# A two-layer diffusion block on TensorE: tile positions, warm matmuls and fp32 modulation sums

## The chip, the cores and the metric

The kernel runs on one core of a Trainium2 chip. The metric is the device time of one execution in microseconds; the median of several runs is compared. TensorE (PE) multiplies matrices and transposes, VectorE (DVE), ScalarE (ACT) and GpSimd (POOL) work on elements, and the transfers from memory run on 16 DMA engines. Two queues issue nearly all transfers: SyncE's (SP), with the weights of the products, and GpSimd's, with the modulation weights and small tables.

## The reference

Two layers of a block over 256 latent and 256 context tokens of width 1024. Each has two sub-layers: a token mixer of three branches (retention, neighbourhood attention, grouped-query attention), merged with gates and projected, and an MLP of width 4096 with a squared ReLU. Every sub-layer is normalised ahead and behind, and modulated by six vectors per layer (two shifts, two scales, two gates), for the latent from c and for the context from c_ctx. The second layer computes the context only as far as the latent reads it. The output is the latent stream.

```
for l in range(2):
    sh1, sc1, gt1, sh2, sc2, gt2 = split(silu(c) @ w_mod[l] + b_mod[l])     # context: the same from c_ctx
    h = rms_norm(x, g_pre_mix[l]) * (1 + sc1) + sh1
    y, yc = token_mixer(h, hc, ...)                                          # w_in, branches, w_br, w_out
    x = x + gt1 * rms_norm(y, g_post_mix[l])
    h = rms_norm(x, g_pre_mlp[l]) * (1 + sc2) + sh2
    x = x + gt2 * rms_norm(square(relu(h @ w_mlp_in[l])) @ w_mlp_out[l], g_post_mlp[l])
    # layer 0 does the same for the context
```

## The kernel before

**Products.** Every large product is computed from two parts of each operand, a high part rounded to fp32r and the rest, in three fp32r matmuls: high by high, high by low, low by high (`mm3`, line 184). The weights come as tiles of 512 KB on SP's queue (`wload`, line 224), ScalarE copies the high part `wh`, and VectorE subtracts for the low part `wl` (`wsplit`, line 230). `wr`, `wh` and `wl` have three buffers each, which are taken in turn. One weight tile is one step of TensorE: 24 matmuls of 512 columns (512 tokens, or 512 weight columns), or 24 of 256 where only the latent is left. In the records such a matmul is named by its output: `ps` (projections and the first MLP product; the weights are held in the array and hT moves), `pO` (second MLP product and w_out; weights move), `pB` and `br` (weights move too).

**Where tiles lie.** Each pool lies behind the one before it in a partition: constants, a pad of `PAD` fp32 columns, 31 S tiles of 4096 bytes (`S`, all large activations: hT, u, yT, z, X, acc), 8 T tiles of 2048 bytes, small tiles, a second pad, the weight buffers. With the sizes declared before, S and T tiles begin 256 bytes past a multiple of 512. A `wh` or `wl` buffer has 1056 columns, 4224 bytes, which is 128 past a multiple of 512; so the three buffers of `wh` begin at 256, 384 and 0 and those of `wl` at 128, 256 and 384. For 256-wide products the weights begin 64 bytes into their buffer (`odd`).

**Order.** Steps are written as a list, and a scheduler orders the instructions of each engine by a modelled timeline with that list as priority. Some are pinned: `Ordered` (line 61) keeps the program's order for instructions issued while it is on, `issue_after` holds an instruction behind another. `HLD` = 2 holds the splits of the first two weight tiles of layer 1's MLP behind `st["xn_ins"]`, the last multiply of the norm.

**Start of layer 1's MLP.** After the last step of w_out (`pO<-wh,yT`), `post` (line 539) updates X per 128 tokens with a chain of eight small VectorE operations (`qv`, `qy`, `qa`). `pre_sq` squares X on ScalarE for each 128 tokens, `pre_xn` (line 499) runs one chain of 14 small operations (`pv`, `py`, `pa`) for both, then multiplies twice: z = X·y. `pre_tr` transposes z on TensorE (16 matmuls into `ph`), `pre_h` makes hT from it, and the MLP's first products follow.

**Modulation sums.** `mod_dve` (line 401) computes one vector: eight tiles `mr` of 128 weight rows come on GpSimd's queue, and VectorE accumulates them into `acc`, one S tile per stream. The first accumulation adds `brow`, a constant tile that is zero but for row 0, into which the bias is written by a transfer. What is left is the sum over the 128 partitions. `fin1` splits `acc` into `ahi` and `alo`. For a gate `fin2` sums with a matrix of ones. For the other vectors it multiplies with `oneh` (a column of ones at the stream's place) into `pmr`, two rows for the two streams, per half of 512 columns; ScalarE copies the two rows to `r`, and `fin3` transposes them by four tiny matmuls per half (`pm<-ident,r`) so that the vector lies along the partitions. Six vectors are non-gates: four for both streams, two for the latent alone. The steps of the modulation are woven between steps of the mixer and of the MLPs.

Of the kernel before, what the change touches and what calls it, by code (L numbers as in the profile page):

```python
# [42 lines left out]
PEO = ((99, 99), (99, 99))  # L43
HLD = 2
GAPF = 0
MPE = False
# [5 lines left out]
PLD = 4  # L52
PAD, PAD2 = 16, 16
FILL = (((0, 9), (9, 21), (21, 33)), ((0, 9), (7, 22), (22, 39)))
# [27 lines left out]
def kernel(  # L82
# [120 lines left out]
    cs = const.tile([128, 8, 2], F32, tag="cs", name="cs")  # L203
    brow = const.tile([128, 2, 512], F32, tag="brow", name="brow")
    ones = const.tile([128, 128], F32R, tag="ones", name="ones")
    oneh = const.tile([128, 2, 128], F32R, tag="oneh", name="oneh")
    onesf = const.tile([128, 128], F32, tag="onesf", name="onesf")
# [11 lines left out]
    def wtile(pool, tag, name, odd=False):  # L219

        t = pool.tile([128, 1056], F32R, tag=tag, name=name)
        return t[:, 16:1040] if odd else t[:, 0:1024]
# [20 lines left out]
    def prologue():  # L243
# [29 lines left out]
        def init():  # L273
            msr = S("msr")
            v_.tensor_copy(msr[:, 0, :], brow[:, 0, :])
            v_.tensor_copy(msr[:, 1, :], brow[:, 0, :])
            msr = msr.rearrange("p a b -> p (a b)").rearrange("p (k m) -> p k m", k=8)
            v_.tensor_copy(msr[:, :, 0:2], cs)
            tt(msr[:, :, 2:4], cs, f(msr[:, :, 0:2]), ALU.subtract)
            M["msr"] = msr  # L280
            for n_ in ("sh1", "sc1"):
                st[0, n_] = smp.tile([128, 8, 2], F32, tag=n_, name=n_, bufs=2)
            pr.extend(mmt(f"pr{i}") for i in range(4))
# [117 lines left out]
    def mod_dve(l, vec, streams):  # L401
# [10 lines left out]
        def fin2():  # L412
            if gate:
                for s in streams:
                    G = S(f"G{s}", F32)
                    st[l, name, s] = G
                    for half in range(2):
# [8 lines left out]
                        tt(G[:, half, :], pg, st["gb", half], ALU.mult)  # L426
                return
            ns = len(streams)
            M["r"] = []
            for half in range(2):  # L430
                ps = att("pmr")
                for s in streams:
                    for p in range(2):
                        t_.matmul(ps, oneh[:, s, :], M[s][p][:, half, :],
                                  start=(s == 0 and p == 0), stop=(s == ns - 1 and p == 1))
                r = T("r2")
                s_.copy(r[0:2, :], ps[0:2, :])
                M["r"].append(r)

        def fin3():  # L440
            o = smp.tile([128, 8, 2], F32, tag=name, name=name, bufs=2)
            st[l, name] = o
            pt = att("pm")
            for half in range(2):
                for j in range(4):
                    jj = 8 * half + 2 * j
                    t_.transpose(pt[:, jj:jj + 2], M["r"][half][0:2, 128 * j:128 * j + 128], ident[0:2, 0:2])
            pt3 = pt[:, 0:16].rearrange("p (j e) -> p j e", e=2)
            for s in streams:
                if vec in (0, 3):  # L450
                    v_.tensor_copy(o[:, :, s], pt3[:, :, s])
                else:
                    stt(o[:, :, s], pt3[:, :, s], 1.0, gp[:, 2 * l + vec // 3, :], ALU.add, ALU.mult)

        def step(kc):
            def go(ws):
                w = mrp.tile([128, 2, 512], F32, tag="mr", name="mr")
                nc.gpsimd.dma_start(  # L458
                    out=w, in_=w_mod[l, 128 * kc:128 * kc + 128, vec * D:vec * D + D].rearrange("p (a n) -> p a n", a=2))
                if kc == 0:  # L460
                    nc.gpsimd.dma_start(out=brow[0:1], in_=b_mod[l:l + 1, vec * D:vec * D + D].rearrange("o (a n) -> o a n", a=2))
                for s in streams:
                    if kc == 0:
                        st["acc", s] = S("acc", F32)
                    a = st["acc", s]
                    stt(a, w, cs[:, kc, s:s + 1], brow if kc == 0 else a, ALU.mult, ALU.add)
            return go

        fins = [fin1, fin2] if gate else [fin1, fin2, fin3]
        o = [([], step(kc)) for kc in range(8)]  # L470
# [28 lines left out]
    def pre_xn(s, sq):  # L499
        ms, z = sq  # L500
        X = st["X"]
        y = stats(ms, 2, EPS, "p")
        st["xn", s] = []
        for t in range(2):
            st["xn_ins"] = v_.tensor_scalar_mul(out=z[t], in0=X[2 * s + t], scalar1=y[:, t:t + 1])
            st["xn", s].append(z[t].rearrange("p a b -> p (a b)"))
# [767 lines left out]
    def setup():  # L1274
# [3 lines left out]
        nc.gpsimd.dma_start(out=sel, in_=sel_in)  # L1278
        v_.memset(brow, 0.0)
        th = sm("cth", 8, 2)  # L1280
# [4 lines left out]
    def setup2():  # L1285
# [9 lines left out]
        v_.tensor_copy(ones, onesf)  # L1295
        v_.tensor_copy(oneh[:, 0, :], brow[:, 0, 0:128])
        v_.tensor_copy(oneh[:, 1, :], brow[:, 0, 0:128])
        v_.tensor_copy(oneh[:, 0, 0:1], onesf[:, 0:1])
        v_.tensor_copy(oneh[:, 1, 1:2], onesf[:, 0:1])

# [60 lines left out]
    pb = pre_steps(1, 1, 0)  # L1361
    steps += pb[:1] + ([([], barrier)] if HLD else []) + pb[1:]
    if MPE:
# [139 lines left out]
```

## Time and profile before

| what | value |
|---|---|
| runs, us | 1471.29, 1471.39, 1478.82 |
| median, us | 1471.39 |
| profiled execution, us | 1478.93 |
| its span, us | 1477.2 |
| granted TensorE clock, mean | 0.990 |
| PE busy, us (share) | 1427.6 (97%) |
| DVE busy, us (share) | 1079.4 (73%) |
| ACT busy, us (share) | 747.1 (51%) |

The span goes from the first to the last instruction of the profiled execution; its own time is 1.7 us longer. Matmuls follow each other more closely than the duration of one record, so that a pace is read from starts or from windows, not from a mean duration. A granted clock of 1.00 is the higher of TensorE's two levels, 2.4 GHz; 0.50 is 1.2 GHz.

### The profile page before, as it was taken

Reading aid. Unit: us, or ns where it says so; the run is one execution under the profiler, and the core shown is the slowest. Engines: PE = TensorE matmul, PEld = TensorE weight load, DVE = VectorE, ACT = ScalarE, POOL = GpSimd, SP = SyncE. Lnnn points to the kernel's source line nnn. Section 1 sums busy time; section 2 is a strip of 40 time slices with the busy share of each in tenths; the row PEclk is TensorE's granted clock in tenths of the full one; section 3 lists DMA queues with packets and bytes.
Section 4 is the critical chain, followed back from the end, with each engine's and each line's share of the span. In section 5 each row is a group of like instructions: output and inputs, shape, how many; then the busy total and the mean of one; then the engine's idle time right before and its main releaser. Section 6 shows DMA issues by size and latency. Waiting matters only on the chain. (4 is left out here: it accounts for less than half of the span.)

```text
span 1477.2 us, 20910 instructions
## 1 busy us (share of the span) xinstructions
PE 1427.6 (97%) x7926; PEld 1212.9 (82%) x7926; DVE 1079.4 (73%) x1999; ACT 747.1 (51%) x1259; POOL 67.8 (5%) x131
## 2 busy tenths in 40 slices
PE   4999999999999999999999999999999999799997
PEld 4878788877788889988888887788889999699886
DVE  5785797787998669967755647986877886766544
ACT  5563565554323347625335155665546655576542
POOL 2000000000110000100001100000000000000000
PEclk9999999999999999999999999999999999899999
DMA  8622121222566556846546647443233445387653
GB/s 287 197 72 72 44 72 58 83 70 91 171 188 183 157 200 174 251 144 188 159 135 218 198 119 235 144 124 95 72 94 107 150 140 189 113 227 215 209 185 119
DMA packets 231957, 219.64 MB, mean 149 GB/s; under 512 B 7652, under 2 KB 188956, under 8 KB 231856
## 3 DMA queue, kind: packets, MB, share of 16 engines
q1 hardware_dynamic: 217856, 170.42, 37.4%
q0 software_dynamic: 14000, 47.88, 10.6%
q8 instruction: 62, 1.02, 0.3%
q14 instruction: 39, 0.32, 0.1%
HBM read 217.22 MB, written 1.05 MB: 148 GB/s over the span
## 5 line engine op out<-in xcount | busy, mean ns | idle before, releaser
L73 PE MATMUL ps<-hT,wh 128*128 128x256 f32 (+1 forms) x2480 | 602.4, 335 | 1.6 <-ACT wh L73 1.6
L73 ACT CAST wh<-wr 128x1024 fp32r<-128x1024 f32 x295 | 309.2, 1051 | 449.9 <-PE ps L73 180.9
L73 DVE TENSOR_TENSOR wl<-wr,wh 128x1024 fp32r<-128x1024 f32 x295 | 359.7, 1223 | 211.7 <-ACT wh L73 211.4
L73 PEld LDWEIGHTS ps<-hT,wh 128*128 128x128 f32 x2480 | 419.1, 190 | 55.5 <-issue 6.6
L73 PE MATMUL ps<-hT,wl 128*128 128x256 f32 (+1 forms) x1240 | 415.2, 335 | 5.1 <-DVE wl L73 4.9
L73 PEld LDWEIGHTS ps<-hT,wl 128*128 128x128 f32 x1240 | 234.9, 189 | 29.2 <-DVE wl L73 6.1
L73 PE MATMUL pO<-wh,u 128*128 128x512 f32 x768 | 241.7, 394 | 0.0
L73 PEld LDWEIGHTS pO<-wh,u 128*128 128x128 f32 x768 | 144.1, 188 | 33.7
L73 DVE SCALAR_TENSOR_TENSOR acc<-mr,cs,acc 128x1024 f32<-128x1024 f32 x112 | 141.2, 1282 | 28.9 <-DMA mr<-in_w_mod_dram 28.4
L73 PE MATMUL pO<-wl,u 128*128 128x512 f32 x384 | 151.2, 394 | 0.2 <-DVE wl L73 0.2
L73 PEld LDWEIGHTS pO<-wl,u 128*128 128x128 f32 x384 | 72.1, 188 | 16.6 <-DVE wl L73 0.6
L73 PE MATMUL pB<-wh,hT 128*128 128x512 f32 x256 | 82.9, 394 | 0.0
L458 POOL DMA_DIRECT2D mr<-in_w_mod_dram x80 | 42.6, 533 | 647.4 <-DVE acc L73 618.5
L73 PE MATMUL pO<-wh,yT 128*128 128x512 f32 x192 | 60.3, 393 | 0.0
L73 PEld LDWEIGHTS pB<-wh,hT 128*128 128x128 f32 x256 | 48.1, 188 | 10.6
L73 DVE TENSOR_TENSOR PT<-pt,PT 128x512 fp32r<-128x512 f32 x80 | 51.5, 682 | 2.8 <-ACT PT L73 2.2
L73 PE MATMUL pB<-wl,hT 128*128 128x512 f32 x128 | 50.3, 393 | 0.0
L73 ACT CAST PT<-pt 128x512 fp32r<-128x512 f32 x80 | 43.2, 599 | 8.5 <-PE pt L73 6.5
L73 PE MATMUL pt<-ident,P 128*128 128x128 f32 x320 | 42.0, 273 | 0.8 <-DVE P L73 0.6
L73 PEld LDWEIGHTS pO<-wh,yT 128*128 128x128 f32 x192 | 35.9, 188 | 8.2
L73 DVE TENSOR_TENSOR u<-rl,u 128x256 fp32r<-128x256 f32 (+1 forms) x71 | 36.7, 517 | 7.4 <-ACT u L73 7.4
L73 DVE TENSOR_SCALAR P<-P,su 128x512 f32<-128x512 f32 (+1 forms) x96 | 40.3, 440 | 1.6
(261 smaller groups left out, 1909.6 us busy)
## 6 DMA issues: line engine op xcount, KB each, us to landing
wr<-in_w_m_dram SPq DMA_DIRECT2D x143, 512.0 KB, 4.5
wr<-in_w_in_dram SPq DMA_DIRECT2D x104, 512.0 KB, 3.7
mr<-in_w_mod_dram POOLq DMA_DIRECT2D x80, 512.0 KB, 4.5
wr<-in_w_br_dram SPq DMA_DIRECT2D x24, 512.0 KB, 3.4
wr<-in_w_out_dram SPq DMA_DIRECT2D x24, 512.0 KB, 3.7
pr<-in_w_mod_dram SPq DMA_DIRECT2D x16, 512.0 KB, 6.3
bt<-in_relb_dram POOLq DMA_DIRECT2D x16, 192.0 KB, 2.7
X<-in_x_dram SPq DMA_DIRECT2D x4, 512.0 KB, 4.9
```

The lines of the kernel that those rows point to most:

```text
L73: ins = call(*a, **k)
L458: nc.gpsimd.dma_start(out=w, in_=w_mod[l, 128 * kc:128 * kc + 128, vec * D:vec * D + D].rearrange("p (a n) -> p a n", a=2))
```

## The change

Four things are done at once. After the last step of w_out in layer 1, `keep_warm` issues 64 matmuls of 256 columns (ones by a tile of yT) into a PSUM tile that nobody reads; the last w_out step, these matmuls and the following transposes are pinned in program order on TensorE. `pre_xn` computes the norm's chain for each 128 tokens by itself, each followed by its multiply, in all its uses. For the non-gate vectors of the modulation `fin1` is gone: `fin2` multiplies `acc` in fp32 with a matrix of 32 columns whose first is ones, one matmul per stream and half, each into a group of 32 PSUM partitions; one ScalarE copy takes all rows, and `fin3` transposes 64 or 128 rows at a time and picks the columns. The bias row lies in an S tile that GpSimd clears for each vector. And the positions change: the constants lose 4992 bytes, `PAD` grows by 1664, `PAD2` by 1024, and `wh` and `wl` buffers by 384 bytes each, so that S and T tiles begin at multiples of 2 KB and all weight buffers at multiples of 512 bytes (256-wide weights still 64 bytes further).

```diff
--- before.py
+++ after.py
@@ -42,6 +42,7 @@
 SWAP = (0, 1)
 PEO = ((99, 99), (99, 99))
 HLD = 2
+WARM1 = 64
 GAPF = 0
 MPE = False
 M1A, M1B = 8, 40
@@ -50,7 +51,7 @@
 ORD = ((0, 4, 5), (0, 4, 8))
 RW = 2
 PLD = 4
-PAD, PAD2 = 16, 16
+PAD, PAD2, WP = 432, 272, 1152
 FILL = (((0, 9), (9, 21), (21, 33)), ((0, 9), (7, 22), (22, 39)))
 PLAN = ["c4 t0 a0 c5 r0 f0 h0 c9 g0 c13",
         "a1 t1 r1 c14 f1 h1 c18",
@@ -201,9 +202,8 @@
     selr = const.tile([4, 512], F32R, tag="selr", name="selr")
     cc = const.tile([128, 8, 2], F32, tag="cc", name="cc")
     cs = const.tile([128, 8, 2], F32, tag="cs", name="cs")
-    brow = const.tile([128, 2, 512], F32, tag="brow", name="brow")
     ones = const.tile([128, 128], F32R, tag="ones", name="ones")
-    oneh = const.tile([128, 2, 128], F32R, tag="oneh", name="oneh")
+    oneh = const.tile([128, 32], F32, tag="oneh", name="oneh")
     onesf = const.tile([128, 128], F32, tag="onesf", name="onesf")
     gp = const.tile([128, 4, 8], F32, tag="gp", name="gp")
     gq_gain = const.tile([128, 4], F32, tag="gain", name="gain")
@@ -218,7 +218,7 @@
 
     def wtile(pool, tag, name, odd=False):
 
-        t = pool.tile([128, 1056], F32R, tag=tag, name=name)
+        t = pool.tile([128, WP], F32R, tag=tag, name=name)
         return t[:, 16:1040] if odd else t[:, 0:1024]
 
     def wload(spec):
@@ -272,8 +272,10 @@
 
         def init():
             msr = S("msr")
-            v_.tensor_copy(msr[:, 0, :], brow[:, 0, :])
-            v_.tensor_copy(msr[:, 1, :], brow[:, 0, :])
+            zero = T("zero")
+            v_.memset(zero, 0.0)
+            v_.tensor_copy(msr[:, 0, :], zero)
+            v_.tensor_copy(msr[:, 1, :], zero)
             msr = msr.rearrange("p a b -> p (a b)").rearrange("p (k m) -> p k m", k=8)
             v_.tensor_copy(msr[:, :, 0:2], cs)
             tt(msr[:, :, 2:4], cs, f(msr[:, :, 0:2]), ALU.subtract)
@@ -425,32 +427,34 @@
                         t_.matmul(pg, ones, M[s][1][:, half, :], start=False, stop=True)
                         tt(G[:, half, :], pg, st["gb", half], ALU.mult)
                 return
+
             ns = len(streams)
-            M["r"] = []
+            ps = att("pmr")
             for half in range(2):
-                ps = att("pmr")
                 for s in streams:
-                    for p in range(2):
-                        t_.matmul(ps, oneh[:, s, :], M[s][p][:, half, :],
-                                  start=(s == 0 and p == 0), stop=(s == ns - 1 and p == 1))
-                r = T("r2")
-                s_.copy(r[0:2, :], ps[0:2, :])
-                M["r"].append(r)
+                    j = 32 * (ns * half + s)
+                    t_.matmul(ps[j:j + 32, :], oneh, st["acc", s][:, half, :], start=True, stop=True)
+            for s in streams:
+                st.pop(("acc", s))
+            r = M["r"] = T("r2")
+            s_.copy(r[0:64 * ns, :], ps[0:64 * ns, :])
 
         def fin3():
             o = smp.tile([128, 8, 2], F32, tag=name, name=name, bufs=2)
             st[l, name] = o
             pt = att("pm")
-            for half in range(2):
-                for j in range(4):
-                    jj = 8 * half + 2 * j
-                    t_.transpose(pt[:, jj:jj + 2], M["r"][half][0:2, 128 * j:128 * j + 128], ident[0:2, 0:2])
-            pt3 = pt[:, 0:16].rearrange("p (j e) -> p j e", e=2)
+            ns = len(streams)
+            R = 64 * ns
+            for j in range(4):
+                t_.transpose(pt[:, R * j:R * j + R], M["r"][0:R, 128 * j:128 * j + 128], ident[0:R, 0:R])
+            p5 = pt[:, 0:4 * R].rearrange("p (j h s e) -> p h j s e", j=4, h=2, s=ns)
             for s in streams:
+                os, ps = o[:, :, s].rearrange("p (h j) -> p h j", h=2), p5[:, :, :, s, 0]
                 if vec in (0, 3):
-                    v_.tensor_copy(o[:, :, s], pt3[:, :, s])
+                    v_.tensor_copy(os, ps)
                 else:
-                    stt(o[:, :, s], pt3[:, :, s], 1.0, gp[:, 2 * l + vec // 3, :], ALU.add, ALU.mult)
+                    g = gp[:, 2 * l + vec // 3, :].rearrange("p (h j) -> p h j", h=2)
+                    stt(os, ps, 1.0, g, ALU.add, ALU.mult)
 
         def step(kc):
             def go(ws):
@@ -458,15 +462,17 @@
                 nc.gpsimd.dma_start(
                     out=w, in_=w_mod[l, 128 * kc:128 * kc + 128, vec * D:vec * D + D].rearrange("p (a n) -> p a n", a=2))
                 if kc == 0:
-                    nc.gpsimd.dma_start(out=brow[0:1], in_=b_mod[l:l + 1, vec * D:vec * D + D].rearrange("o (a n) -> o a n", a=2))
+                    M["b"] = S("brow", F32)
+                    nc.gpsimd.memset(M["b"], 0.0)
+                    nc.gpsimd.dma_start(out=M["b"][0:1], in_=b_mod[l:l + 1, vec * D:vec * D + D].rearrange("o (a n) -> o a n", a=2))
                 for s in streams:
                     if kc == 0:
                         st["acc", s] = S("acc", F32)
                     a = st["acc", s]
-                    stt(a, w, cs[:, kc, s:s + 1], brow if kc == 0 else a, ALU.mult, ALU.add)
+                    stt(a, w, cs[:, kc, s:s + 1], M["b"] if kc == 0 else a, ALU.mult, ALU.add)
             return go
 
-        fins = [fin1, fin2] if gate else [fin1, fin2, fin3]
+        fins = [fin1, fin2] if gate else [fin2, fin3]
         o = [([], step(kc)) for kc in range(8)]
         for g in fins:
             o += [([], lambda ws, g=g: g())] + [([], lambda ws: None)] * GAPF
@@ -499,10 +505,10 @@
     def pre_xn(s, sq):
         ms, z = sq
         X = st["X"]
-        y = stats(ms, 2, EPS, "p")
         st["xn", s] = []
         for t in range(2):
-            st["xn_ins"] = v_.tensor_scalar_mul(out=z[t], in0=X[2 * s + t], scalar1=y[:, t:t + 1])
+            y = stats(ms[:, t:t + 1], 1, EPS, "p")
+            st["xn_ins"] = v_.tensor_scalar_mul(out=z[t], in0=X[2 * s + t], scalar1=y[:, 0:1])
             st["xn", s].append(z[t].rearrange("p a b -> p (a b)"))
         if s == 0:
             st["hT"] = [None] * 8
@@ -1276,7 +1282,6 @@
         nc.gpsimd.dma_start(out=ident, in_=ident_in)
         nc.gpsimd.dma_start(out=gp, in_=gpre)
         nc.gpsimd.dma_start(out=sel, in_=sel_in)
-        v_.memset(brow, 0.0)
         th = sm("cth", 8, 2)
         s_.activation(th, cc, AF.Tanh, scale=0.5)
         stt(th, th, 1.0, cc, ALU.add, ALU.mult)
@@ -1293,10 +1298,8 @@
         v_.tensor_copy(selr, sel4[0:4])
         v_.memset(onesf, 1.0)
         v_.tensor_copy(ones, onesf)
-        v_.tensor_copy(oneh[:, 0, :], brow[:, 0, 0:128])
-        v_.tensor_copy(oneh[:, 1, :], brow[:, 0, 0:128])
-        v_.tensor_copy(oneh[:, 0, 0:1], onesf[:, 0:1])
-        v_.tensor_copy(oneh[:, 1, 1:2], onesf[:, 0:1])
+        v_.tensor_scalar_mul(out=oneh, in0=onesf[:, 0:32], scalar1=0.0)
+        v_.tensor_copy(oneh[:, 0:1], onesf[:, 0:1])
 
         a, b, e, p = sm("lga", 16), sm("lgb", 16), sm("lge", 16), sm("lgp", 16)
         ts(a, lgt, -1.0, None, ALU.mult, ALU.bypass)
@@ -1359,7 +1362,23 @@
     steps += m1_[1 + NB2:]
     steps += wout_steps(1, 0)
     pb = pre_steps(1, 1, 0)
-    steps += pb[:1] + ([([], barrier)] if HLD else []) + pb[1:]
+
+    def own(step):
+        def go(ws):
+            t_.own = True
+            step[1](ws)
+            t_.own = False
+        return (step[0], go)
+
+    def keep_warm(ws):
+
+        w = att("warm")
+        for _ in range(WARM1):
+            t_.matmul(w[:, 0:256], ones, st["yT"][7][0], start=True, stop=True)
+
+    steps[-1] = own(steps[-1])
+    steps += [own(([], keep_warm))]
+    steps += pb[:1] + ([([], barrier)] if HLD else []) + [own(p) for p in pb[1:]]
     if MPE:
         steps += mod_pe(1, 5)
         steps += mlp_steps(1, [])
```

## Rows read from the trace of the kernel before

**Rows 1.** The page's head, and busy time of each engine with its instructions.

```profile
span 1477.2 us, 20910 instructions
...
PE 1427.6 (97%) x7926; PEld 1212.9 (82%) x7926; DVE 1079.4 (73%) x1999; ACT 747.1 (51%) x1259; POOL 67.8 (5%) x131
```

**Rows 2.** Windows: length, busy PE, PEld, DVE, ACT, POOL; clock, DMA share, GB/s.

```profile
100.00:900.00 800.00, 798.47 (x3928) 653.52 (x3927) 591.69 (x967) 369.03 (x619) 49.19 (x93) 1.00 0.47 143
```

**Rows 3.** Windows cut at weight steps (overlapping neighbours are counted too).

```profile
722.99:728.59 5.60, 5.60 (x26) 4.51 (x25) 5.20 (x5) 1.05 (x1) 1.05 (x2) 1.00 0.66 190
728.59:734.10 5.51, 5.51 (x25) 4.50 (x24) 5.07 (x6) 1.05 (x1) 0.53 (x1) 1.00 0.91 305
734.10:739.69 5.59, 5.59 (x25) 4.50 (x24) 5.39 (x5) 1.05 (x1) 0.53 (x1) 1.00 0.42 115
...
787.19:792.74 5.55, 5.55 (x25) 4.54 (x24) 3.98 (x4) 2.80 (x5) 0.62 (x3) 1.00 0.65 197
809.39:814.89 5.50, 5.50 (x26) 4.50 (x24) 1.22 (x1) 1.05 (x1) 0.00 (x0) 1.00 0.30 93
...
865.92:871.53 5.61, 5.61 (x26) 4.51 (x24) 3.14 (x3) 3.75 (x6) 0.00 (x0) 1.00 0.31 96
1362.42:1365.14 2.72, 2.72 (x26) 2.72 (x25) 1.59 (x3) 2.15 (x4) 0.00 (x0) 1.00 0.71 184
```

**Rows 4.** Timeline, MLP start in layer 1: start, duration, instruction, idle before in brackets.

```profile
1273.43 0.15 DVE L73 TENSOR_SCALAR qv<-zms 128x1 f32<-128x1 f32 x1
...
1275.16 1.28 DVE L73 SCALAR_TENSOR_TENSOR X<-z,qy,X 128x1024 f32<-128x1024 f32 x1
1277.66 0.17 DVE L73 TENSOR_SCALAR pv<-pms 128x2 f32<-128x2 f32 x1 [1.22 <-ACT z L73]
...
1279.44 1.41 DVE L73 TENSOR_SCALAR z<-X,py 128x1024 f32<-128x1024 f32 x2
1280.76 2.35 DVE L73 TENSOR_TENSOR wl<-wr,wh 128x1024 fp32r<-128x1024 f32 x2
...
1280.33 3.65 PE L73 MATMUL ph<-ident,z 128*128 128x128 f32 x16 [9.39 <-DVE z L73]
1283.63 0.99 PE L73 MATMUL ps<-hT,wh 128*128 128x256 f32 x3
```

**Rows 5.** Windows, the 5 us in which TensorE starts layer 1's MLP.

```profile
1280.00:1285.00 5.00, 4.67 (x24) 4.60 (x25) 5.00 (x12) 3.12 (x7) 0.00 (x0) 0.54 0.26 72
```

**Rows 6.** PE groups by form: names, shapes, count, busy us, mean ns, idle.

```profile
L73 PE MATMUL ps<-hT,wh 128*128 128x512 f32 x1136 | 362.4, 398 | 0.0
L73 PE MATMUL pO<-wh,u 128*128 128x512 f32 x768 | 241.7, 394 | 0.0
...
L73 PE MATMUL pB<-wh,hT 128*128 128x512 f32 x256 | 82.9, 394 | 0.0
L73 PE MATMUL pO<-wh,yT 128*128 128x512 f32 x192 | 60.3, 393 | 0.0
...
L73 PE MATMUL br<-yret,wh 128*128 128x512 f32 x64 | 20.9, 405 | 0.0
```

**Rows 7.** Timeline of PE, modulation sums of one vector for both streams.

```profile
761.97 0.39 PE L73 MATMUL pmr<-ahi,oneh 128*128 128x512 f32 x1
...
763.83 0.40 PE L73 MATMUL ps<-hT,wh 128*128 128x512 f32 x1
764.16 0.40 PE L73 MATMUL pm<-ident,r 2*128 2x2 f32 x4
764.50 0.50 PE L73 MATMUL ps<-hT,wh 128*128 128x512 f32 x1
764.83 0.39 PE L73 MATMUL ps<-hT,wl 128*128 128x512 f32 x1
```

**Rows 8.** Groups by form on PE: fp32 transposes, and fp32 products of the prologue.

```profile
L73 PE MATMUL pt<-ident,P 128*128 128x128 f32 x320 | 42.0, 273 | 0.8 <-DVE P L73 0.6
...
L73 PE MATMUL pm<-sel,r 5*128 5x2 f32 x32 | 5.0, 274 | 0.7 <-ACT r L73 0.7
```

## The prediction

> **What bounds the kernel now.** I read the page first. TensorE is busy for 1427.6 of the 1477.2 us of the span, the next engine, VectorE, for 1079.4 [rows 1]. The windows then show that this is no average over unlike stages: from 100 to 900 us TensorE has work for 798.47 of 800 us, at the full granted clock [rows 2]. So in that stretch nothing is gained by a wait that some other engine no longer has; time goes only if TensorE gets fewer instructions or each takes less. Two kinds of stretch are left: the pace of the matmuls themselves, and the few places where TensorE stands still.
>
> For the pace I cut the span at the bounds of weight steps. A step is one 512 KB weight tile: 24 matmuls of 512 columns. With the clock at 1.00 in every row, no step waits, and yet they are not equal: 5.60, 5.51, 5.59, 5.55, 5.50, 5.61 us [rows 3]. The first three are neighbours of one kind (pO), and go through the three buffers of the pool in turn (wh/wl at 256/128, 384/256, 0/384 bytes past a multiple of 512); the same three lengths come back in the same order. The other engines don't explain it: the short step of 5.51 us has VectorE busy for 5.07 us and the DMAs at 0.91, the one of 5.60 us has 5.20 and 0.66 [rows 3]. I read this as an effect of where the operands lie.
>
> For the standstills, the largest late one is at the start of layer 1's MLP: TensorE waits 9.39 us for z before 16 transposes [rows 4], and comes back at half the clock: 0.54 granted in the mean over the next 5 us [rows 5], that is mostly the lower of its levels, 1.2 GHz, where it had 2.4.
>
> **The change part by part.** The sums are made against the profiled execution, 1478.93 us (its span is 1477.2); the median of the three runs shown is 7.54 lower, 1471.39, and I carry the difference over to that. About 0.5%, 7.4 us, is what a measurement of this kernel can tell from no change: under 1464.0 is faster, over 1478.8 slower.
>
> *A, the place of the tiles.* The 512-wide products of this kind are 1136, 768, 256, 192 and 192 with a high half of the weights, and half as many again with the low half [rows 6]: 2544 × 1.5 = 3816 matmuls = 159 steps. The six steps average 5.56 us. Afterwards S tiles, T tiles and weights all begin at a multiple of 512 bytes. Two of the six rows are near that: 728.59, where the moving low half shares the place of the S tiles (256), takes 5.51, and 809.39, where the high half does, 5.50. I take 5.50 for all: 159 × (5.50 − 5.56) = −9.5 us. Bounds: the fastest row of the trace is a step of 24 matmuls of 256 columns, 2.72 us [rows 3], so 5.44 for 512: −19.1 us. At the slow end stands the row 865.92, a step of the other kind (ps, hT moving and the weights held) with its low half at 256 too: 5.61, where its neighbour in another buffer takes 5.55. If that is what a shared place does, it is 159 × 0.05 = +8.0. With each kind at its own row (88 pO-like steps at 5.51 against their mean 5.567, 71 at 5.61 against 5.57, the mean of 5.55 twice and 5.61) the result is −5.0 + 2.8 = −2.2.
>
> *B, the start of layer 1's MLP.* Now VectorE ends X at 1276.4, idles 1.22 us for the squares, runs one chain of 14 small operations for both halves (1277.66 to 1279.44), then both multiplies, 1.41 us [rows 4]; behind them stand the two held weight subtractions (2.35 us from 1280.76) and the first hT, and the products start at 1283.63. With a chain per 128 tokens, the first half's chain and multiply need only the first half's square and fit into the idle 1.22 us and what lies before it. The second half needs 8 small operations, as many as the chain from 1273.43 to 1275.16 takes, 1.73 us [rows 4], and one multiply, about 0.7: 1277.66 + 1.73 + 0.70 = 1280.1 instead of 1280.85. That is −0.7; if nothing of the first half fits ahead, the two chains stand one after the other and it is +1.7 − 0.7 = about +1. In the other three uses VectorE has slack or waits for a transfer: 0, and a few tenths if that cover is gone. The 64 warm matmuls of 256 columns take 64 × 2.72/24 = 7.3 us [rows 3], and lie in the 9.39 us of waiting; they end near 1278.3, so they delay nothing unless the wait shrinks by over 2 us. What they give back is little, since what follows the 16 transposes is paced by VectorE's subtractions: only the first four products at half speed, −0.5. If the clock falls back in the 2 us that are left, that is 0. B = −1.2, between −3 (the transposes' 3.65 us halved and the rest following) and +1. Pinning the last output step, the warm matmuls and the transposes in program order adds no wait: in the trace they run in that order with nothing between.
>
> *C, the sums of the modulation.* Six non-gate vectors, four for both streams and two for the latent alone. Before, one of the first sort costs TensorE eight matmuls from 761.97 to 763.83, 1.86 us, and two groups of four tiny transposes; one of those, with the changes between data types, takes 764.83 − 763.83 less two products of 0.233, 0.54 [rows 7]. So 1.86 + 2 × 0.54 = 2.94, with half the matmuls 2.01: 4 × 2.94 + 2 × 2.01 = 15.8 us. Afterwards there are four (two) fp32 matmuls of 512 columns into groups of 32 columns, and four transposes of 128 (64) rows. fp32 products appear in the trace as pairs: 16 written ones are 32 records [rows 8]. The nearest row for an fp32 pass is the transpose of 128 columns, 42.0/320 = 0.131 us [rows 8], 0.52 for 512. If the four groups run at the same time, two passes are about 0.9–1.0; one after another, eight are 4.2. I take the middle of 0.9 and 3.5 (with 0.44 a pass, as the same records give without their changeover), 2.2, since no row shows groups of columns. With changeovers of 0.2 twice and four transposes of 0.13: 3.1 (1.8 to 5.1). For the latent alone, 2.1 (1.6 to 3.0). Sum 4 × 3.1 + 2 × 2.1 = 16.6: C = +0.8, between −5.4 and +10.6. By the Trainium skill, "TensorE: Matmul & The Clock Gate", Part 3, "Measured speedup vs the span model", three groups of 32 columns at N = 512 ran 2.38 times as fast as one by one; by that, as an estimate, the sums of 3.5 would shrink to 1.5 and C to −2. No row here shows it either way.
>
> *The rest.* Ten splits fewer, each one ACT copy and one VectorE subtraction, are off TensorE's path in the stretch of 798.47 of 800 [rows 2]: 0. The bias row moves to an S tile that GpSimd clears ahead of the same transfer; GpSimd may wait there for a free S tile, and behind it stand the weight rows of the same vector, for which VectorE's accumulations wait, and the weight subtractions behind those. No row shows this wait; TensorE's idle 1.5 us in the 800 of [rows 2] says that such waits are covered now: 0, and a few us once if a slot is late. Clearing "zero" on VectorE in the prologue replaces clearing a row of the same sort: 0.
>
> Sum: −9.5 − 1.2 + 0.8 = −9.9. From 1478.93 that is 1469.0 for the profiled execution, and 1461.5 for the median.
>
> **The rivals.** *R2, the place is nothing.* The steps differ for another reason (the PSUM bank, or the order of products), A = 0: −0.4, 1471.0. For it: among pO steps 809.39 is as short as 728.59 though its buffer is that of 722.99, which is long [rows 3]. Against it: the three lengths that come back with the three buffers. The Trainium skill, "SBUF — State Buffer", section "Who interferes with whom", has the rule that speaks for R2: PE waits on no one, and its moving and weight reads are independent. The trace does not bear it out fully, with 5.51 beside 5.60.
>
> *R3, the fp32 sums run one after another.* C is +10.6 and eats A: −9.5 − 1.2 + 10.6 = −0.1, 1471.3. For it: fp32 products come as pairs of records [rows 8]. Against it: four separate groups of columns that share no output.
>
> *R4, slower: the shared place is the slow one.* All steps go to the 5.61 of row 865.92: +8.0 − 0.4 = +7.6, 1479.0. It decides as soon as a step takes over 5.563 (A over +0.4), and shows as slower from 5.609 on. For it: in the ps kind the buffer at the S tiles' place is the longest. Against it: in the pO kind it is the shortest, and those are the more.
>
> **How the numbers follow.** The forecast, A at 5.50 with B and C at their values, has 0.58; its own range is 1455 to 1469, from 5.46 a step to −2.2 for A, and nearly four fifths of it lie under 1464. R2 has 0.22, R3 0.10, R4 0.10. Faster by over 0.5% is 0.45 from the forecast and 0.03 from R2 and R3 with C at its low end: 0.48. Slower by over 0.5% is most of R4: 0.07. The rest, 0.45, is the same. The range must take in R2 and R3 with C some us up, and below it the fast bound of A in part: 1453 (5.45 a step, −17.5, with −0.9 from the rest) to 1474. R4 is left out.
>
> **What the profile after would show.** A is right if the steps of 24 no longer differ by buffer and take 5.50 or less, pO and ps alike, over the 159; wrong if the three lengths stay (R2) or all go to 5.60 and more (R4). B is right if TensorE is busy up to about 1278 on the old scale, the transposes follow at a clock of 1.00, and the products start about 0.7 us sooner after the last X; wrong if the transposes wait behind the warm matmuls. C is right if the fp32 sums of one vector for both streams take near 2.2 us; under 1.2 the groups run together, over 3.5 R3 holds. The prediction as a whole fails first through A: 0.05 us a step is the whole of the forecast.

## The result, and the profile after

The kernel after takes 1462.09 us in the median of five runs (1458.87 to 1463.87), the one before 1471.39. The ratio is 0.9917, with a 95% interval of 0.9895 to 0.9938. In a second set of runs it was 0.9941 (0.9920 to 0.9961). The forecast was 1461.5.

The total is where it was expected, but not by the terms that were expected. The page's head and its busy line, of the kernel after (the profiled execution; before: [rows 1]):

```profile
span 1460.7 us, 21002 instructions
...
PE 1414.4 (97%) x7966; PEld 1209.2 (83%) x7966; DVE 1070.0 (73%) x2001; ACT 733.1 (50%) x1243; POOL 77.6 (5%) x141
```

The spans differ by 16.5 us, the medians by 9.3: the profile of before is of an execution 7.5 us above its median. To see where, I cut both traces at the first matmul of each weight tile, counted in TensorE's order (295 tiles in both), and followed by how much the kernel after is ahead:

| at tile | before, us | after, us | ahead | gained since the row above |
|---|---|---|---|---|
| 1 | 72.69 | 70.92 | 1.77 | 1.8 |
| 145 | 903.81 | 887.12 | 16.69 | 14.9 |
| 169 | 996.37 | 989.92 | 6.45 | −10.2 |
| 229 | 1262.47 | 1255.98 | 6.49 | 0.0 |
| 235 | 1292.45 | 1284.81 | 7.64 | 1.2 |
| 253 | 1348.21 | 1333.77 | 14.44 | 6.8 |
| 295 | 1464.29 | 1447.89 | 16.40 | 2.0 |

The 6.8 us between tiles 235 and 253 are stalls in the profiled execution of before, the largest of them at 1343.35: TensorE waited 2.69 us for a weight subtraction, and the clock fell to its lower level for 6.8 us (a second profile of before, below, takes 3.9 us less in this stretch). Without the 6.8 us 9.6 are left, near the medians' 9.3. In the stretch with 0.0, layer 1's mixer and w_out, what the wide steps gain goes to those of 256 columns (below). The row to explain is the third: 10.2 us, three fifths of what had been gained, are lost between the end of layer 0's MLP and the start of layer 1, called the boundary below.

**Steps.** Windows at the bounds of weight steps, of the kernel after (columns as in [rows 2]); a pO step, a ps step, and a step of 256 columns:

```profile
710.74:716.18 5.44, 5.44 (x25) 4.50 (x24) 4.83 (x5) 1.06 (x1) 0.77 (x2) 1.00 0.83 277
839.04:844.48 5.44, 5.44 (x25) 4.51 (x24) 1.92 (x2) 2.80 (x5) 0.00 (x0) 1.00 0.42 121
1284.81:1287.53 2.72, 2.72 (x26) 2.72 (x25) 2.23 (x4) 2.69 (x5) 0.00 (x0) 1.00 0.65 184
```

Of the 80 steps of 24 wide matmuls that run in one piece, 60 take 5.44 us, in both kinds and in every buffer. Before, none was under 5.49. (The 159 steps of the prediction are wide matmuls counted by 24. A weight tile of w_out or of the second MLP product is only 12 of them where it meets 256 tokens.)

**Modulation sums.** Timeline of TensorE in the kernel after, one vector for both streams; above the "..." the sums, below it the transposes of another such vector:

```profile
692.48 0.39 PE L74 MATMUL ps<-hT,wl 128*128 128x512 f32 x1
692.80 1.06 PE L74 MATMUL pmr<-acc,oneh 128*32 128x512 f32 x8
693.79 0.73 PE L74 MATMUL ps<-hT,wh 128*128 128x512 f32 x2
...
750.71 0.63 PE L74 MATMUL ps<-hT,wh 128*128 128x512 f32 x2
751.18 0.60 PE L74 MATMUL pm<-ident,r 128*128 128x128 f32 x4
751.53 0.48 PE L74 MATMUL ps<-hT,wl 128*128 128x512 f32 x1
751.85 0.63 PE L74 MATMUL ps<-hT,wh 128*128 128x512 f32 x2
```

Eight records (four fp32 products, two each) take 693.79 − 692.48 less one product of 0.227, 1.08 us, where the split sums took 1.86 [rows 7]. For the latent alone four records, half as many, stand there for the same time:

```profile
855.46 1.05 PE L74 MATMUL pmr<-acc,oneh 128*32 128x512 f32 x4
856.44 0.73 PE L74 MATMUL ps<-hT,wh 128*128 128x512 f32 x2
```

So the groups of 32 columns run side by side: four cost what two cost, and eight records one after another would take 1.8 us even at the 0.227 of the wide fp32r products. The transposes take 751.85 − 750.71 less three products, 0.46 us, in place of two groups of 0.54.

**Start of layer 1's MLP.** Timeline of the kernel after (before: [rows 4]), and two windows (before: [rows 5]):

```profile
1264.14 7.68 PE L74 MATMUL warm<-yT,ones 128*128 128x256 f32 x64
1271.66 0.27 PE L74 MATMUL ph<-ident,z 128*128 128x128 f32 x1
1273.61 1.86 PE L74 MATMUL ph<-ident,z 128*128 128x128 f32 x15 [1.68 <-DVE z L74]
1275.23 0.60 PE L74 MATMUL ps<-hT,wh 128*128 128x256 f32 x3
1276.61 0.39 PE L74 MATMUL ps<-hT,wh 128*128 128x256 f32 x1 [0.79 <-DVE hT L74]
...
1268.58 1.28 DVE L74 SCALAR_TENSOR_TENSOR X<-z,qy,X 128x1024 f32<-128x1024 f32 x1
1270.22 0.76 DVE L74 TENSOR_SCALAR z<-X,py 128x1024 f32<-128x1024 f32 x1
1272.80 0.76 DVE L74 TENSOR_SCALAR z<-X,py 128x1024 f32<-128x1024 f32 x1
```

```profile
1268.00:1273.00 5.00, 3.93 (x34) 3.69 (x32) 4.55 (x20) 1.15 (x2) 0.00 (x0) 1.00 0.00 0
1273.00:1278.00 5.00, 3.60 (x30) 3.40 (x31) 4.89 (x12) 3.76 (x8) 0.00 (x0) 1.00 0.38 101
```

The clock stays at its upper level, the first z is out before the second half's chain begins, and what is left of the wait is 1.68 and 0.79 us, both for VectorE.

### The profile page after: what moved, and what is told of

Same layout as the page of the kernel before. It is cut to its first block, busy times and chain, and to the rows that moved or that the text cites. A ratio compares the mean times of both kernels' runs of the same rounds, so it can differ in the third digit from the quotient of the medians.

```text
span 1460.7 us, 21002 instructions
## 1 busy us (share of the span) xinstructions
PE 1414.4 (97%) x7966; PEld 1209.2 (83%) x7966; DVE 1070.0 (73%) x2001; ACT 733.1 (50%) x1243; POOL 77.6 (5%) x141
## 4 chain that ended last, share of the span: by engine, by line
PE 83%; DVE 6%; issue 4%; DMA 4%; ACT 2%; SPq 0%; POOL 0%; DVEq 0%; ACTq 0%; POOLq 0%
PE ps L74 37%; PE pO L74 17%; PE br L74 7%; PE pB L74 6%; PE po L74 3%; PE pt L74 2%; PE sl L74 2%; DVE wl L74 2%; PE pr L74 2%; PE gkv L74 2%; DMA wr<-in_w_m_dram 1%; DMA pr<-in_w_mod_dram 1%; DVE hT L74 1%; PE ro L74 1%; PE modps L74 1%
## 5 line engine op out<-in xcount | busy, mean ns | idle before, releaser
L74 PE MATMUL pO<-wh,u 128*128 128x512 f32 x768 | 238.5, 390 | 0.0
```

The costliest lines, as they stand in the source:

```text
L74: ins = call(*a, **k)
```

## The experiments

All ratios are to runs of the kernel before on the same chip, whose median went from 1471 to 1477 us from one set to another; so runs of different sets are compared by ratio.

**The kernel before again**, unchanged.

> The kernel before, unchanged, for a second profile. Its runs fall on two levels (1470.7 to 1471.4, and 1477.9 to 1478.8), and the profile shown is of the upper one. Theory 1: the 7.4 us between them are one stall in layer 1's MLP (from 1340.7 on in the trace: 2.9 us of waiting and 6.8 us at half the clock); a profile of about 1471 lacks it and agrees with the first elsewhere within 1 us. Rival: the levels differ in the pace of the steps (over the 159 steps 0.05 us each); then a profile of 1471 has steps of about 5.51 in the mean.

Measured: 1475.95 us. At tile 145 it stands 1.6 us behind the first profile, at tile 235 1.5 behind, at 253 2.4 ahead: the stall is down to a wait of 0.9 us with no fall of the clock. The steps are the same (mean of 84 steps 5.577 in both). The difference between these two is stalls and falls of the clock, not pace; but it is more than one stall, since this execution takes 1476 us without the large one. The two levels themselves did not hold: 17 more executions spread from 1471 to 1480 us.

**Place and bias row alone, all but the place, and the old sums in the new place.**

```
e1:  mod_dve as before, but brow an S tile cleared on GpSimd; pre_xn as before; no keep_warm, no own
     PAD, PAD2, WP = 208, 272, 1152          # S, T, wr, wh, wl at 0 mod 512, as after
e2:  the kernel after with  PAD, PAD2, WP = 1264, 16, 1056   # every tile where it lay before
e4:  e1 with the norms per 128 tokens, keep_warm and own
```

> Tile positions of the kernel after and its bias row in an S tile, nothing else: sums in split fp32r, one norm chain for both halves, no warm matmuls. Both theories: every undisturbed step of 24 takes 5.44 us, so about 159 x (5.44 - 5.56) = -19 us before waits. Theory 1 (the loss of some 10 us between 890 and 968 us in the kernel after belongs to the new order of the modulation's steps, with its sums in fp32): that stretch has under 3 us of new idle time, and the time is 1453 to 1456. Theory 2 (TensorE's lead is eaten there whatever made it, since the weight transfers and VectorE set the pace): the idle time comes back, and the time is 1462 to 1466. If place does nothing: 1471.

> The kernel after with the tiles where they lay before (S tiles at 256 past a multiple of 512, weight buffers of 4224 bytes), the rest as after. All theories: steps of 5.49 to 5.61 as before. Theory 1 (the loss belongs to the order of the modulation's steps): the sums give back 6 to 7 us, the MLP's start 1 to 2, and the loss of about 10 us stays: 1471 to 1476. Theory 2 (the loss is TensorE's lead eaten): without the lead no loss, 1461 to 1465.

> The kernel after with the modulation's sums as before (split into two fp32r parts, eight matmuls and eight tiny transposes per vector); the bias row's S tile, the place, the norms and the warm matmuls stay. Sums: TensorE pays about 15.8 us for them instead of about 9. Theory 1 (the loss at 890 to 968 belongs to the new order): the loss goes with it: about 1462 + 6.8 - 10 = 1459 or less, down to 1453. Theory 2 (lead eaten, whatever made it): the loss stays but is smaller by what the sums now take: 1462 to 1466.

Measured: e1 1466.18, ratio 0.9940 (0.9919 to 0.9961). e2 1476.61, 1.0006 (0.9989 to 1.0023). e4 1467.73, 0.9946 (0.9928 to 0.9965). Windows from tile 109 to tile 145 and from there to tile 169, of the kernel before, e1, e2, and the kernel after, each in a fence:

```profile
705.54:903.81 198.27, 198.27 (x870) 160.23 (x868) 117.99 (x120) 73.00 (x98) 19.81 (x38) 1.00 0.56 174
903.81:996.37 92.56, 87.72 (x465) 73.41 (x464) 80.42 (x192) 56.33 (x92) 0.21 (x1) 1.00 0.49 152
```

```profile
698.10:892.37 194.27, 194.27 (x869) 159.81 (x868) 114.26 (x117) 73.26 (x97) 21.45 (x38) 1.00 0.56 173
892.37:986.69 94.32, 87.44 (x465) 73.13 (x464) 83.62 (x195) 55.98 (x91) 1.59 (x3) 1.00 0.51 158
```

```profile
704.77:903.28 198.51, 197.05 (x860) 157.69 (x857) 111.35 (x114) 70.22 (x93) 20.41 (x36) 1.00 0.54 164
903.28:1005.60 102.32, 92.57 (x462) 76.24 (x461) 83.36 (x198) 54.14 (x89) 2.12 (x4) 0.95 0.51 155
```

```profile
693.79:887.12 193.33, 193.03 (x861) 157.39 (x857) 111.37 (x114) 70.34 (x93) 20.42 (x36) 1.00 0.55 169
887.12:989.92 102.80, 91.30 (x461) 76.39 (x460) 83.20 (x198) 54.33 (x89) 2.12 (x4) 0.95 0.50 154
```

In both profiles of the kernel before the second stretch takes 92.56 us. Of the 10.2 us that the kernel after loses there, 6.7 are idle time of TensorE (11.50 us against 4.84); the rest is longer busy time at a lower granted clock, 0.95 in the mean where before has 1.00. The place, with the bias row's tile, takes 4.0 us off the first stretch, 0.11 for each of its 36 tiles, and adds 1.8 to the second. All but the place leaves the first as it was and adds 9.8 to the second; at tile 145 TensorE was then 0.5 us ahead of the first profile of before and 2.1 ahead of the second. So the loss at the boundary does not come from TensorE's lead (theory 2 falls); it comes with the new sums (theory 1). In e4, with the lead, the norms per 128 tokens and the old sums, the second stretch takes 95.71, 7.1 less than in the kernel after.

By the totals the whole gain is that of the place (with the bias row's tile): e1 has 0.9940, the kernel after 0.9917 and 0.9941, and e2, with everything else, 1.0006. What the other parts save is lost again at the boundary. The total times don't separate the theories as I had set them: I had counted the place at 19 us and nothing against it. What e1 lacks is in the steps of 256 columns. Of 67 such steps 45 take 2.72 us in the second profile of before (44 in the first); in e1 none does, and 64 take 2.83 to 2.94, about 5 us in all. In e2, with every tile where it lay before, about as many take 2.72 as in the kernel before, and its wide steps keep their lengths:

```profile
716.39:721.98 5.59, 5.59 (x25) 4.51 (x24) 4.78 (x6) 1.05 (x1) 1.09 (x2) 1.00 0.58 154
727.58:733.10 5.52, 5.52 (x26) 4.50 (x24) 3.94 (x5) 1.05 (x1) 0.12 (x1) 1.00 0.51 156
```

**The kernel after again, and the modulation woven over fewer steps.** The list of steps shows what the sums have to do with the boundary. In VectorE's order the last vector's last accumulation stands behind 147 weight subtractions; in the kernel before behind 144, in e1 and e4, with the bias row's S tile alone, behind 146. `fin1` is gone, so a non-gate vector has 10 steps instead of 11, and the weave spreads 60 instead of 64 over the same MLP. The edit: `MLB = 10` in place of 2 (135 subtractions).

> The kernel after, unchanged, beside the next three on the same chip, and for a second profile. Both theories: about 0.992 of the time before; idle time of over 8 us between 885 and 960 us, as in the first profile.

> The kernel after with the modulation steps of layer 0's MLP woven over fewer of its steps (MLB 10 instead of 2): the last accumulation for the last vector stands behind 135 weight subtractions in VectorE's order, instead of 147 (144 in the kernel before). Theory 1 (the loss at the layer boundary is made by this late vector, whose rows and sums meet the second MLP product): the idle time between 885 and 960 us falls below 4 us, the time by 7 to 10 us, to about 1453 to 1456 or 0.986 of before. Rival (VectorE's own work at the boundary, norms and subtractions, is what TensorE's lead runs into): idle time stays within 2 us, 0.992.

Measured: after again 1465.24, 0.9941 (0.9920 to 0.9961); woven earlier 1462.81, 0.9935 (0.9919 to 0.9950): no difference that can be told. The same two stretches in the run woven earlier:

```profile
692.89:897.43 204.54, 197.70 (x861) 159.09 (x860) 117.04 (x117) 71.74 (x94) 22.50 (x40) 0.98 0.57 175
897.43:987.34 89.91, 84.22 (x454) 71.92 (x452) 77.72 (x192) 54.01 (x88) 0.00 (x0) 1.00 0.47 142
```

The boundary's loss is gone (89.91 is shorter than before; the last sums have left the stretch too, 454 matmuls in place of 461); and the stretch ahead of it is 11 us longer. Neither theory had that: the loss moves with the modulation's steps. Timeline of that run, TensorE's longest wait there and VectorE ahead of it:

```profile
746.58 0.69 PE L74 MATMUL ps<-hT,wh 128*128 128x512 f32 x2 [2.87 <-DVE z L74]
...
743.41 1.28 DVE L74 SCALAR_TENSOR_TENSOR acc<-mr,cs,acc 128x1024 f32<-128x1024 f32 x1 [2.75 <-DMA mr<-in_w_mod_dram]
744.62 1.22 DVE L74 TENSOR_TENSOR wl<-wr,wh 128x1024 fp32r<-128x1024 f32 x1
745.75 1.28 DVE L74 TENSOR_TENSOR z<-z,pO 128x512 f32<-128x512 f32 x2
```

VectorE stands 2.75 us in front of an accumulation whose weight rows have not landed; behind it, in its fixed order, stand a subtraction and the reads of pO that free TensorE's PSUM banks. VectorE is the engine with time to spare, and here it still decides when TensorE goes on. At the boundary of the kernel after VectorE waits for rows as well. But what TensorE's wait there ends with is a late weight tile: `wh` is ready at 894.25 and `wl` starts at 894.40, so that without the wait for rows `wl` could have started only 0.15 us sooner:

```profile
892.60 1.28 DVE L74 SCALAR_TENSOR_TENSOR acc<-mr,cs,acc 128x1024 f32<-128x1024 f32 x1 [2.60 <-DMA mr<-in_w_mod_dram]
893.80 0.68 DVE L74 TENSOR_TENSOR z<-z,pO 128x512 f32<-128x512 f32 x1
894.40 1.22 DVE L74 TENSOR_TENSOR wl<-wr,wh 128x1024 fp32r<-128x1024 f32 x1
...
893.21 1.04 ACT L74 CAST wh<-wr 128x1024 fp32r<-128x1024 f32 x1 [4.84 <-DMA wr<-in_w_m_dram]
...
895.67 0.50 PE L74 MATMUL pO<-wl,u 128*128 128x512 f32 x1 [2.73 <-DVE wl L74]
```

**Three buffers for the rows**, as they are and woven earlier. If late rows in front of VectorE are the cause, a third buffer lets a transfer start one accumulation sooner.

```
e9:   tc.tile_pool(name="mrp", bufs=3)      # 2 before; NS = 30 (31) pays for it
e10:  the same, and MLB = 6                 # last accumulation behind 141 subtractions
```

> The kernel after with three buffers for the modulation's weight rows instead of two, and 30 S tiles instead of 31 in exchange. Theory 1, as it stands now: VectorE, which works in order, waits for late rows (30 us in 23 waits), and the drains and subtractions behind such an accumulation make TensorE wait, at the layer boundary or wherever the rows are put. Then these waits fall to under 15 us, TensorE's idle time between 885 and 960 us halves, and the time is 1457 to 1460 where the kernel after has 1462 to 1465. Rival: the transfers themselves are the limit (their share is 0.8 in those stretches); then the waits stay at 25 us and more, and the time at 1462 or above; above it too if 30 S tiles are too few.

> As the run with three buffers, and the modulation steps woven over fewer steps of layer 0's MLP (MLB 6 instead of 2), so that the last vector ends about six weight steps sooner. Theory 1: both places of loss shrink, 1453 to 1457. Rival (the loss only moves with the rows, since the transfers are the limit): 1461 to 1465.

Measured: three buffers 1462.19, 0.9897 (0.9880 to 0.9914); woven earlier too 1456.11, 0.9859 (0.9846 to 0.9872), the fastest kernel of this study. The first missed the expected 1457 to 1460 in time, though not by its ratio (the kernel before stands at 1476.93 beside it), and the ratio can't be told from the 0.9917 of the kernel after (0.9895 to 0.9938). The second came as expected, and its ratio can. VectorE's waits for the rows (us in all, times, longest), in the kernel after and in the run with three buffers:

```profile
DVE acc L74 <- DMA mr<-in_w_mod_dram: 30.2, 23, 2.6
```

```profile
DVE acc L74 <- DMA mr<-in_w_mod_dram: 10.2, 10, 1.9
```

The two stretches of the fastest run, and the second one with three buffers alone:

```profile
695.70:890.54 194.84, 194.53 (x861) 157.11 (x860) 116.93 (x117) 71.77 (x94) 21.02 (x38) 1.00 0.58 185
890.54:980.17 89.63, 84.34 (x453) 72.04 (x452) 77.68 (x192) 54.02 (x88) 0.00 (x0) 1.00 0.46 139
```

```profile
888.94:988.05 99.11, 90.62 (x462) 76.37 (x460) 82.37 (x197) 54.28 (x89) 1.58 (x3) 0.95 0.50 157
```

In the fastest run both are short at once: 284.5 us together, against 296.1 in the kernel after, 294.4 woven earlier with two buffers and 290.8 before. The third buffer alone did not do that. I had expected it to halve the idle time at the boundary, and 8.5 of 11.5 us are left; 99.11 us also lies within what kernels with two buffers and the same order of the modulation take there, from 97.09 (e8) to 102.80. And VectorE waits for rows in that stretch for only 0.6 us, where it waited 3.7 in the kernel after. So most of the boundary's loss, 6.6 of 10.2 us, stands almost without such waits.

What stays with the loss are late weight tiles. ScalarE's waits for tiles of the MLP's weights in the second stretch, in the kernel after and with three buffers:

```profile
ACT wh L74 <- DMA wr<-in_w_m_dram: 16.0, 5, 5.8
```

```profile
ACT wh L74 <- DMA wr<-in_w_m_dram: 4.9, 3, 2.6
```

In both runs woven earlier there are none, in the kernel before one of 4.4 us. The late tile of 893.21 took 6.6 us from issue to landing, with rows under way beside it; in the fastest run, where the rows are through, the eight tiles issued from 882.9 to 904.0 took 3.5 to 3.9. That transfers of the rows hold up the weight tiles fits this, but no run tried it alone. Nor is it shown what the third buffer does in the fastest run, which has `MLB = 6` where e6 has 10: no run has 6 with two buffers.

**Parts of term B.** No warm matmuls and no pinning (e7); one norm chain for both halves, as before (e8).

> The kernel after without the 64 warm matmuls and without the pinning of TensorE's order around them; norms per 128 tokens stay. By the prediction's term B the warm matmuls are worth 0.5 us: 1462.5. Rival: they keep the clock at its upper level for the whole start of the MLP, and without them a stretch of 10 us at half the clock costs 3 us: 1465. If they cost anything: below 1461.5.

> The kernel after with one chain of small operations for both halves of 128 tokens in every norm, as before. By term B: 0.7 us longer at the start of layer 1's MLP, 1462.8. Theory 1: the idle time at the layer boundary stays (over 8 us). Rival to it: the chains per 128 tokens, two for one, load VectorE at the boundary and make the loss; then that idle time falls to under 4 us and the time to 1454 to 1457.

Measured: e7 1464.93, 0.9937 (0.9913 to 0.9961); e8 1463.71, 0.9943 (0.9926 to 0.9959); the kernel after beside them 0.9941. Neither part can be told from nothing by the total. In the traces it can: from the first matmul of tile 231 (w_out's last) to tile 235 the kernel before takes 25.83 us, after 24.75, and without warm matmuls 25.63, all three with 256-wide steps of 2.72 us. The runs with steps of 2.83: after again 24.86, with the old norm 25.56. So the warm matmuls give 0.9 us and the chains 0.7, each beside the other; together they give 1.1, not the sum. The window of the run without warm matmuls shows the clock that they keep up:

```profile
1269.80:1274.80 5.00, 3.60 (x18) 3.15 (x17) 4.79 (x13) 1.96 (x5) 0.00 (x0) 0.50 0.05 13
```

At the layer boundary the run with the old norm takes 97.09 us. Runs with the kernel after's order of instructions and other shifts take 97.85 and 98.06, so this does not show that the chains load the boundary; it stays open.

**Which place counts.** Everything shifted by 256 bytes (`PAD` 496), and only the weight buffers shifted (`PAD2` 336); one run each.

> The kernel after with S tiles, T tiles and weight buffers all shifted by 256 bytes. Theory P1 (what counts is that held and moving operands lie at the same place modulo 512): undisturbed steps of 24 stay at 5.44 us. Rival P2 (what counts is the place itself, a multiple of 512): they go to 5.5 to 5.6 us, and the time up by 10 us or more.

> The kernel after with S and T tiles at multiples of 512 and all weight buffers 256 bytes further. Theory P1 (the same place of both operands counts): steps of 5.5 to 5.6 us, in both kinds. Rival P3 (it counts only that the buffers of weights do not differ among themselves): 5.44 us.

Measured: 1462.13 and 1458.70 us. A pO and a ps step of the first run, and of the second:

```profile
710.50:715.94 5.44, 5.44 (x25) 4.50 (x24) 5.32 (x5) 1.06 (x1) 0.53 (x1) 1.00 0.81 276
665.72:671.16 5.44, 5.44 (x26) 4.50 (x24) 5.44 (x6) 2.80 (x5) 0.53 (x1) 1.00 0.81 247
```

```profile
710.07:715.51 5.44, 5.44 (x26) 4.50 (x25) 5.33 (x5) 1.06 (x1) 0.53 (x1) 1.00 0.81 267
670.70:676.14 5.44, 5.44 (x25) 4.50 (x24) 4.88 (x6) 2.80 (x5) 1.06 (x2) 1.00 0.78 224
```

So neither a multiple of 512 (P2) nor the same place of both operands (P1) counts. What the kernel before has and none of these has is a weight buffer 128 bytes off, against the other one and against the S tiles. Whether it is that offset between buffers (P3), or a start that is no multiple of 256 bytes, was not tried apart.

## Why the prediction came out

**A: right in sign, mis-sized, and for a wrong reason.** The step that failed is "I take 5.50 for all". Steps went to 5.44, the bound taken from a step of 256 columns; by 4.0 us in 36 tiles (e1) the 159 steps are worth some −17.7 us, not −9.5. The reason, that the weights would share the place of the S tiles, fell with e12. R2 and R4 fall with the rows at 5.44; the rule of the Trainium skill behind R2 ("SBUF — State Buffer", "Who interferes with whom") does not cover this: the measured steps, 5.49 to 5.61 in e2 against 5.44 in the kernel after with only the addresses changed, decide. And the term left out the 256-wide steps, whose price the new place raises: 45 of 67 at 2.72 us became 28 in one profile of the kernel after and none in the other, 2 to 5 us.

**B: right.** −1.2 was forecast, 1.1 us were measured up to tile 235. Taken out alone, the norm's share came as forecast (0.7) and the warm matmuls' was more (0.9, forecast 0.5); the two overlap, which the sum had not foreseen.

**C: wrong in sign.** "I take the middle of 0.9 and 3.5": the four groups run at the same time, 1.08 us with changeovers, so the lower end was the right one. Between the same tiles of e4 and of the kernel after again, a vector for both streams costs 1.0 to 1.3 us less, four of them some −4.8, and the one for the latent that can be compared nothing: about −5 in all, the end of the bounds (−5.4) and not +0.8. R3 falls. The packing figure of the Trainium skill ("TensorE: Matmul & The Clock Gate", "Measured speedup vs the span model"), 2.38 for three groups, pointed the right way; here four fp32 products take 1.08 us against an estimate of 3.5 one by one from the transposes' rows.

**The rest, "0, and a few us once": the term that failed most.** The mechanism was named there, accumulations that block the subtractions behind them, but for a missing S tile and as a rare case. It was the order: the last rows come three weight steps later, two by the bias row's tile and one with the new sums, into the boundary, and 9 to 10 us were lost between tiles 145 and 169 (e2, after, after again). That the loss hangs on where the last vector's steps stand is shown by e6 and e10, which move them ahead and have none there. That it is VectorE's waits for rows, as the term had it, is shown only for the waits of e6, ahead of the boundary; at the boundary e9 speaks against it, and late weight tiles are the open rival. Why one weight step, from 146 to 147, costs 7 us more is open too.

So −9.9 was forecast as −9.5 − 1.2 + 0.8, and what came is about −17.7 and +2 to +5 for the place, −1, −5, and +10 for the boundary, −9 to −12. The forecast time is right by luck: two errors of some 8 and 6 us met one of 10 and one of 2 to 5.

## What to carry to other kernels

Where a profile shows steps of several lengths that come back with the buffers, try every buffer at the same offset, and look at each operand width by itself: here the wide steps gained and those of 256 columns lost. The fastest row of the trace was the better forecast here. Taking steps out of a woven list moves all that is left: look where the last piece lands, and what stands behind it in an in-order engine. An engine that is busy for three quarters of the time can still stop the one that is busy for 97%, if it waits for a transfer in front of a read that frees PSUM (2.87 us at once in e6). Moving those rows and giving them a third buffer gave about as much again as the whole change (0.9859 against 0.9917 and 0.9941); which of the two did it was not separated.

## What was not expected of the hardware

A step of 24 fp32r matmuls of 512 columns takes 5.49 to 5.61 us (e2) or 5.44 us (the kernel after) by the position of its buffers alone, 229 to 234 or 227 ns a matmul. The 256-wide step has two paces that one and the same program shows in different executions: 2.72 us throughout the first MLP product in the first profile of the kernel after, and in the second one

```profile
1285.14:1287.96 2.82, 2.82 (x26) 2.82 (x25) 2.33 (x4) 2.77 (x5) 0.00 (x0) 1.00 0.64 185
```

for nearly every step of the same stretch, at the same granted clock. The first profile has both paces in one execution: 2.83 us in layer 1's mixer, 2.72 in the MLP behind it. What sets which of the two was not found.
